# The first stage of a hybrid encoder layer written anew: halved first weights, squares behind the next chunk's high halves, additions on VectorE, memory tokens split directly

## The chip, the cores and the metric

The kernel runs on 1 core of one Trainium2 chip. The metric is the device time of one execution in microseconds (us), the median of the runs. The engines are named as in the profile: PE is TensorE (matmuls; PEld its weight loads), DVE VectorE, ACT ScalarE, POOL GpSimd, SP the engine whose queue issues most of the DMAs.

## What is computed

One step of an encoder layer for a prompt of 1024 frames and 8 samples of 16 frames, together 1152 tokens of width 1024, all in float32:

```python
h = rmsnorm(x, p['g_pre1'])              # x * rsqrt(mean(x*x) + 1e-6) * g
z = h @ p['w_in']                        # (1152, 1024) @ (1024, 1024)
u_ssm, u_pool, q_mem = z[..., :512], z[..., 512:768], z[..., 768:]
y_ssm, ... = s5_scan(u_ssm, ...)         # complex diagonal state space
y_pool, ... = multiscale_pool(u_pool, ...)
y_mem = memory_attention(q_mem, mk, mv)
gates = sigmoid(h @ p['w_gate'] + p['b_gate'])       # three branches
x = x + rmsnorm((gates * branches @ w_br).sum() @ p['w_out'], p['g_post1'])
x = x + rmsnorm(conv_ffn(rmsnorm(x, p['g_pre2']), ...), p['g_post2'])

def memory_kv(mem, g_mem, w_mem_k, w_mem_v):         # 256 memory tokens
    mn = rmsnorm(mem, g_mem)
    return mn @ w_mem_k, mn @ w_mem_v
```

The change touches the first RMS norm, the first columns of `z`, and `memory_kv` of the prompt.

## The kernel before

Every float32 operand of a matmul is split into a high half and a low half (`whi`, `wlo` for weights, `hhi`, `hlo` for tokens, `mhi`, `mlo` for memory tokens). The high half is an ACT copy into the type that PE multiplies, the low half is the difference, made on DVE as a rule. `mm3` (L101) makes one product from three matmuls: high by high (L103), weights' high by tokens' low (L106), weights' low by tokens' high (L107).

The tokens lie as features by tokens: 8 tiles of 128 features, in three chunks of 384 tokens. `z_tile(w, c)` (L195) makes 128 columns of `z` for chunk `c`: 8 feature tiles, 24 matmuls of 128x384, in one bank of PSUM. There are four banks called `pc` and four called `ps`.

The norm's gain `g` is put into the tokens when they are split: `feat_split` (L122) makes `hhi` on ACT (L126) and `hlo` on DVE (L127), a feature tile at a time. The norm's factor is put in after the matmul. `feat_sq` (L134) squares a chunk in four pieces of 128x768 (L140 on ACT, L142 on POOL if its letter in `engs` is "G"), adds them in pairs (L144, on POOL), adds the two sums (L148) and the halves of that (L149) on DVE; `feat_cols` (L153) sums over features with six matmuls by a column of ones (L156). `rsqrt` (L80) takes the root (ACT L84, POOL L86), `row_bcast` (L89) makes three diagonal matrices on ACT (L94) and spreads them by matmul (L96), ACT copies that to `rb` (L177), and `scaled` (L198) multiplies a finished tile of `z` by it on DVE (L200), whereupon `done` writes it out by DMA.

`start` (L262) is the first stage: it loads the tokens in 12 pieces (L165) and the weights of columns 0, 1 and 2, makes the nine `z` tiles of them, the three chunks' factors, and then the memory tokens' keys, the tiles of columns 3 (`z(3)`) and the memory tokens' values. Chunk 0's sums are called `q0`, chunk 1's `q1`, chunk 2's `q2`. `mem_split` (L217) multiplies the memory tokens by their gain on POOL (L224), copies the high half on ACT (L63) and subtracts on POOL (L64). Beside it stands `ssm_params` (from L339), many small DVE operations on the state-space parameters (called `pr` in the profile, L356 to L506), which the scheduler sets between the rest.

The order on each engine is made by a scheduler from its own estimate of times. The program steers it in three ways: `keep_in_program_order` (`pin=True`) holds a matmul at its written place among the pinned ones, `high_priority` brings work forward, and `issue_after(i)` keeps all work in its block behind instruction `i`. The raw weights have 3 buffers, the split weights 6, and the squares share 2 buffers of tag `U` and one each of `CA` and `V`.

Of the kernel before, what the change touches and what calls it, by code (L numbers as in the profile page):

```python
# [8 lines left out]
F32R = mybir.dt.float32r  # L9
# [12 lines left out]
V_GPRE1, V_GPRE2, V_GMEM, V_BGATE, V_BGLU = 0, 8, 16, 24, 48  # L22
# [10 lines left out]
class K:  # L33
# [67 lines left out]
    def mm3(self, out, whi, wlo, xhi, xlo, start, stop, pin=False):  # L101
        nc = self.nc
        i = nc.tensor.matmul(out, whi, xhi, start=start, stop=False)  # L103
        if pin:
            self.tc.keep_in_program_order(i)
        nc.tensor.matmul(out, whi, xlo, start=False, stop=False)  # L106
        nc.tensor.matmul(out, wlo, xhi, start=False, stop=stop)  # L107
# [26 lines left out]
    def feat_sq(self, P, x, n, tags, engs="AAAA", add=True):  # L134
        nc = self.nc
        sq = [P.tile([128, 2, n * 128], F32, tag=t, name="sq") for t in tags]
        for a in range(4):
            xa = x[:, 2 * a:2 * a + 2]
            if engs[a] == "A":
                nc.scalar.activation(sq[a], xa, AF.Square)  # L140
            else:
                (nc.vector if engs[a] == "V" else nc.gpsimd).tensor_mul(sq[a], xa, xa)  # L142
            if a % 2:
                nc.gpsimd.tensor_add(sq[a - 1], sq[a - 1], sq[a])  # L144
        parts = [sq[i][:, k] for i in (0, 2) for k in range(2)]
        if add:
            with self.tc.high_priority():
                nc.vector.tensor_add(sq[0], sq[0], sq[2])  # L148
                nc.vector.tensor_add(parts[0], parts[0], parts[1])  # L149
            parts = parts[:1]  # L150
        return parts
# [64 lines left out]

    def mem_split(self, x):  # L217

        nc = self.nc
        mhi = self.mtile([128, 8, 256], F32R, "mhi")  # L220
        mlo = self.mtile([128, 8, 256], F32R, "mlo")
        for a in range(2):
            ks = slice(4 * a, 4 * a + 4)
            nc.gpsimd.tensor_mul(x[:, ks], x[:, ks],  # L224
                                 self.vec[:, V_GMEM + 4 * a:V_GMEM + 4 * a + 4, None].to_broadcast([128, 4, 256]))
            self.split(mhi[:, ks], mlo[:, ks], x[:, ks], nc.gpsimd)
        return mhi, mlo

    def mem_rows(self, P, rs):
# [32 lines left out]
    def start(self, P, pair, done, z):  # L262
        nc = self.nc
        self.hhi, self.hlo = [], []
        sh = (128, 4, 256)
        I = self.I
        x0 = self.h_load(0, (0,))
        rw = [self.load_raw(I["w_in"][pair[0]])]
        self.h_load(0, (1, 2, 3), x0)
        rw.append(self.load_raw(I["w_in"][pair[1]]))  # L270
        x1 = self.h_load(1)
        x2 = self.h_load(2)
        tags = ("U", "U", "CA", "V")
        ss = self.sm()

        def rms(c0, n):
            with self.tc.high_priority():
                return self.rsqrt(P, ss[:, c0:c0 + n], n)

        self.h_tiles()  # L280
        a, v = self.h_split(x0, (0, 1))
        w = [self.load_w(None, r=rw[0])]
        lo, up = range(4), range(4, 8)
        with self.tc.issue_after(a.ins), self.tc.issue_after(v.ins):
            self.h_split(x0, range(2, 8))
            b0 = [self.z_tile(w[0], 0, pin=True)]
            w.append(self.load_w(None, r=rw[1]))
            q0 = self.feat_sq(P, x0, 3, tags, "AGAA")
        self.h_tiles()
        self.h_split(x1)  # L290
        b0.append(self.z_tile(w[1], 0, pin=True))
        t = self.pc()
        self.z_tile(w[0], 1, t, lo, True)
        self.feat_cols(q0, 3, ss[:, 0:3], True)
        b1 = [self.z_tile(w[0], 1, t, up, True)]
        b1.append(self.z_tile(w[1], 1, pin=True))
        self.h_tiles()
        self.h_split(x2, lo)
        self.h_rows(P, rms(0, 3), 0, True)
        with self.tc.issue_after(self.diag.ins):  # L300
            self.h_split(x2, up)
            for i in range(2):
                done(pair[i], 0, b0[i])
            q1 = self.feat_sq(P, x1, 3, tags, add=True)
            t = self.sm()
            self.z_tile(w[0], 2, t, lo, True)
            self.feat_cols(q1, 3, ss[:, 3:6], True)
            b2 = [self.z_tile(w[0], 2, t, up, True)]
            t = self.pc()
            self.z_tile(w[1], 2, t, lo, True)  # L310
            self.h_rows(P, rms(3, 3), 1, True)
            b2.append(self.z_tile(w[1], 2, t, up, True))
            for i in range(2):
                done(pair[i], 1, b1[i])
        with self.tc.issue_after(self.diag.ins):
            w2 = self.load_w(I["w_in"][2])
            q2 = self.feat_sq(P, x2, 3, tags, "AAAA")
            done(2, 0, self.z_tile(w2, 0, pin=True))
            self.feat_cols(q2, 3, ss[:, 6:9], True)
            done(2, 1, self.z_tile(w2, 1, pin=True))  # L320
            b = self.z_tile(w2, 2, pin=True)
            self.h_rows(P, rms(6, 3), 2, True)
            d = self.diag
            for i in range(2):
                done(pair[i], 2, b2[i])
            done(2, 2, b)
            xm = self.mem_load()
            wk = [self.load_w(I["w_mk"][h], sh) for h in range(2)]
            self.feat_sums(P, xm, 2, ss[:, 9:11], tags, "AAAA")
            mem = self.mem_split(xm)  # L330
            rsm = self.mem_rows(P, rms(9, 2))
            self.mem_out(P, "mk", self.mem_kv(mem, "mk", wk), *rsm)
            z(3)
            wv = [self.load_w(I["w_mv"][h], sh) for h in range(2)]
            self.mem_out(P, "mv", self.mem_kv(mem, "mv", wv), *rsm)
        return d
# [1500 lines left out]
```

## Time and profile before

| | |
|---|---|
| median of 3 runs | 1626.8 us (1624.13 to 1631.04) |
| the profiled execution | 1622.7 us, its span 1620.9 us |
| mean granted clock of PE | 0.979 |
| busy: PE, DVE | 1558.3 us (96%), 1031.3 us (64%) |
| busy: ACT, POOL | 586.2 us (36%), 586.3 us (36%) |
| DMA | 163.44 MB, mean 101 GB/s |

The span is the time between the first and the last instruction that the profiler saw. A row of a timeline reads: start, length (both us), engine, line, operation, output and inputs by the program's names, shapes, count; in brackets the idle time of the engine before the row and what ended it. A row of the groups gives the count, the busy time in us and the mean of one in ns.

### The profile page before, as it was taken

To read this page: it belongs to the slowest core of one execution; us is meant where nothing else is said; L and a number is where in the kernel's file an instruction comes from. 1 tells how busy PE (TensorE), PEld (TensorE's weight loads), DVE (VectorE), ACT (ScalarE), POOL (GpSimd) and SP (SyncE) were. 2 spreads that over 40 slices of the span, in tenths; PEclk is the share of its full clock that TensorE was granted. 3 is DMA by queue.
4 is the path that set the end of the run, shared out by engine and by line. 5 is a ranking of instruction groups with operands and counts; after the bars stand their busy time and mean duration, and the time that the engine had idled before them with its cause. 6 is when DMAs were issued, how large, how long until landed. Compare 5 with 4: busy or idle time off the path is not lost.

```text
span 1620.9 us, 22934 instructions
## 1 busy us (share of the span) xinstructions
PE 1558.3 (96%) x8964; PEld 1511.3 (93%) x8964; DVE 1031.3 (64%) x1549; ACT 586.2 (36%) x893; POOL 586.3 (36%) x509
## 2 busy tenths in 40 slices
PE   6899999999999999999879999999999999999996
PEld 5899999868899999998879999999999998999996
DVE  7864987645643354624678655555655658788866
ACT  6322444253321242434445333433333333332321
POOL 2400001000011143326666444534443426655546
PEclk9899999999999999999879999999999999999998
DMA  6343334413232235122323221212121233133214
GB/s 245 100 146 95 107 114 145 150 64 121 95 117 81 71 80 162 56 96 76 122 88 129 76 75 62 82 69 81 54 82 69 82 135 122 51 110 103 91 64 166
DMA packets 98460, 163.44 MB, mean 101 GB/s; under 512 B 23216, under 2 KB 68656, under 8 KB 98352
## 3 DMA queue, kind: packets, MB, share of 16 engines
q1 hardware_dynamic: 97920, 161.75, 30.3%
q8 instruction: 70, 1.15, 0.3%
q14 instruction: 38, 0.31, 0.1%
q10 hardware_dynamic: 432, 0.23, 0.0%
HBM read 119.52 MB, written 42.42 MB: 100 GB/s over the span
## 4 chain that ended last, share of the span: by engine, by line
PE 79%; DVE 9%; issue 3%; DMA 3%; ACT 2%; POOL 1%; POOLq 0%; SPq 0%; DVEq 0%; ACTq 0%
PE pc L107 14%; PE pc L103 14%; PE pc L106 14%; PE ps L103 10%; PE ps L106 10%; PE ps L107 10%; PE ps L842 1%; DVE dB L64 1%; DMA Ts<-DG 1%; POOL ssa L1057 1%; DVE wlo L64 1%; PE ps L1065 1%; DMA DG<-gs 1%; DMA dwr<-in_w_down 1%; DVE mg L1095 1%
## 5 line engine op out<-in xcount | busy, mean ns | idle before, releaser
L103 PE MATMUL pc<-hhi,whi 128*128 128x384 f32 x760 | 259.9, 342 | 7.7 <-ACT hhi L126 7.6
L106 PE MATMUL pc<-hlo,whi 128*128 128x384 f32 x760 | 260.7, 343 | 2.6 <-DVE hlo L127 2.6
L107 PE MATMUL pc<-hhi,wlo 128*128 128x384 f32 x760 | 257.7, 339 | 0.5 <-DVE wlo L64 0.5
L63 ACT ACTIVATE whi<-rawt 128x1024 fp32r<-128x1024 f32 x102 | 107.5, 1055 | 180.7 <-PE pc L106 80.7
L64 DVE TENSOR_TENSOR wlo<-rawt,whi 128x1024 fp32r<-128x1024 f32 x102 | 131.9, 1295 | 56.9 <-ACT whi L63 56.3
L103 PEld LDWEIGHTS pc<-hhi,whi 128*128 128x128 f32 x760 | 144.8, 191 | 10.3 <-ACT hhi L126 7.6
L106 PEld LDWEIGHTS pc<-hlo,whi 128*128 128x128 f32 x760 | 144.7, 190 | 7.4 <-DVE hlo L127 3.5
L107 PEld LDWEIGHTS pc<-hhi,wlo 128*128 128x128 f32 x760 | 144.6, 190 | 3.2 <-issue 1.6
L200 DVE TENSOR_TENSOR sg<-pc,rb 128x384 f32<-128x384 f32 x95 | 52.3, 553 | 122.7 <-PE pc L107 120.2
L107 PE MATMUL pc<-h2hi,wlo 128*128 128x384 f32 x352 | 119.1, 338 | 2.1 <-DVE wlo L64 2.0
L103 PE MATMUL pc<-h2hi,whi 128*128 128x384 f32 x352 | 118.3, 336 | 0.0
L106 PE MATMUL pc<-h2lo,whi 128*128 128x384 f32 x352 | 118.2, 336 | 0.0
L64 DVE TENSOR_TENSOR S<-S,S 128x512 fp32r<-128x512 f32 x85 | 75.9, 895 | 64.2 <-ACT S L63 62.2
L63 ACT ACTIVATE S<-S 128x512 fp32r<-128x512 f32 x88 | 55.1, 629 | 160.2 <-PE ps L107 89.8
L917 ACT ACTIVATE sg<-sg,vec 128x384 f32<-128x384 f32 x72 | 44.1, 613 | 148.2 <-DVE sg L200 121.2
L1004 POOL TENSOR_TENSOR mg<-mg,sgl 128x384 f32<-128x384 f32 x24 | 28.2, 1174 | 171.9 <-DVE sgl L1002 168.6
L103 PE MATMUL ps<-bT,S 128*128 128x384 f32 x240 | 80.2, 334 | 0.0
L106 PE MATMUL ps<-bT,S 128*128 128x384 f32 x240 | 80.2, 334 | 0.0
L107 PE MATMUL ps<-bT,S 128*128 128x384 f32 x240 | 80.2, 334 | 0.0
L1237 POOL TENSOR_TENSOR S<-rawt 128x512 f32<-128x512 f32 x22 | 29.8, 1355 | 125.9 <-PE ps L107 124.3
L63 ACT ACTIVATE dhi<-dwr 128x1024 fp32r<-128x1024 f32 x38 | 39.7, 1058 | 95.9 <-PE pc L106 61.4
L107 PEld LDWEIGHTS pc<-h2hi,wlo 128*128 128x128 f32 x352 | 66.1, 188 | 2.8 <-DVE wlo L64 2.8
(458 smaller groups left out, 4401.0 us busy)
## 6 DMA issues: line engine op xcount, KB each, us to landing
rawt<-in_w_up SPq DMA_DIRECT2D x48, 512.0 KB, 3.3
Dact<-t SPq DMA_DIRECT2D x22, 576.0 KB, 3.5
rawt<-in_w_gate SPq DMA_DIRECT2D x24, 512.0 KB, 3.5
dwr<-in_w_down SPq DMA_DIRECT2D x22, 512.0 KB, 3.5
Dsg<-sg SPq DMA_DIRECT2D x45, 192.0 KB, 1.9
sgl<-Dsg SPq DMA_DIRECT2D x45, 192.0 KB, 2.4
dBr<-Dact SPq DMA_DIRECT2D x8, 768.0 KB, 5.7
xT<-in_xT SPq DMA_DIRECT2D x12, 384.0 KB, 7.6
```

The source lines that it names most:

```text
L63: nc.scalar.activation(hi, src, AF.Copy)
L64: (eng or nc.vector).tensor_sub(lo, src, hi)
L103: i = nc.tensor.matmul(out, whi, xhi, start=start, stop=False)
L106: nc.tensor.matmul(out, whi, xlo, start=False, stop=False)
L107: nc.tensor.matmul(out, wlo, xhi, start=False, stop=stop)
L200: self.nc.vector.tensor_mul(sg, b, self.rb[:, c, :])
L842: nc.tensor.matmul(o, va[:, m, 2 * hp + e, :], pT[:, m, :], start=m == 0, stop=m == 1)
L917: self.nc.scalar.activation(sg, sg, AF.Sigmoid, bias=self.vec[:, V_BGATE + m:V_BGATE + m + 1])
L1004: nc.gpsimd.tensor_add(m, m, sp)
L1057: self.sqadd = G.tensor_add(ss[0], ss[0], sq)
L1065: m = nc.tensor.matmul(s3[:, t:t + 1], s[:, t * 128:t * 128 + 128], self.ones[:, 0:1], start=(i, t) == (0, 0), stop=(i, t) == (len(ss) - 1 ...
L1237: G.tensor_sub(s3, a11, a21)
```

## The change

Five things, all in the first stage. The numbers of lines after the change are two higher from about L270 on.

- The pair additions of the squares (L144) go from POOL to DVE, and all squares of chunk 0 to ACT.
- The memory tokens are split by `feat_split`, as the others are: eight ACT copies with the gain as scale and eight DVE operations of 128x256, and no multiplication by the gain ahead of them.
- The first weights come in two DMAs of four feature tiles each, and are split in two halves, each followed by four feature tiles of chunk 0.
- The squares of a chunk stand behind all high halves of the next chunk, by `issue_after`; before, chunk 0's stood between its own high halves.
- The blocks of `issue_after` are drawn anew: nearly the whole stage stands in the first one, and the memory tokens behind the diagonal of row 1.

```diff
@@ -141,7 +141,7 @@
             else:
                 (nc.vector if engs[a] == "V" else nc.gpsimd).tensor_mul(sq[a], xa, xa)
             if a % 2:
-                nc.gpsimd.tensor_add(sq[a - 1], sq[a - 1], sq[a])
+                nc.vector.tensor_add(sq[a - 1], sq[a - 1], sq[a])
         parts = [sq[i][:, k] for i in (0, 2) for k in range(2)]
         if add:
             with self.tc.high_priority():
@@ -216,14 +216,9 @@
 
     def mem_split(self, x):
 
-        nc = self.nc
         mhi = self.mtile([128, 8, 256], F32R, "mhi")
         mlo = self.mtile([128, 8, 256], F32R, "mlo")
-        for a in range(2):
-            ks = slice(4 * a, 4 * a + 4)
-            nc.gpsimd.tensor_mul(x[:, ks], x[:, ks],
-                                 self.vec[:, V_GMEM + 4 * a:V_GMEM + 4 * a + 4, None].to_broadcast([128, 4, 256]))
-            self.split(mhi[:, ks], mlo[:, ks], x[:, ks], nc.gpsimd)
+        self.feat_split(x, mhi, mlo, V_GMEM, range(8))
         return mhi, mlo
 
     def mem_rows(self, P, rs):
@@ -265,7 +260,10 @@
         sh = (128, 4, 256)
         I = self.I
         x0 = self.h_load(0, (0,))
-        rw = [self.load_raw(I["w_in"][pair[0]])]
+        halves = slice(0, 4), slice(4, 8)
+        rw = [self.rawtile([128, 8, 128])]
+        for hs in halves:
+            nc.sync.dma_start(rw[0][:, hs], I["w_in"][pair[0]][:, hs])
         self.h_load(0, (1, 2, 3), x0)
         rw.append(self.load_raw(I["w_in"][pair[1]]))
         x1 = self.h_load(1)
@@ -279,42 +277,45 @@
 
         self.h_tiles()
         a, v = self.h_split(x0, (0, 1))
-        w = [self.load_w(None, r=rw[0])]
+        w = [[self.w1.tile([128, 8, 128], F32R, tag="w", name=n) for n in ("whi", "wlo")]]
+        self.split(w[0][0][:, halves[0]], w[0][1][:, halves[0]], rw[0][:, halves[0]])
         lo, up = range(4), range(4, 8)
         with self.tc.issue_after(a.ins), self.tc.issue_after(v.ins):
-            self.h_split(x0, range(2, 8))
+            self.h_split(x0, (2, 3))
+            self.split(w[0][0][:, halves[1]], w[0][1][:, halves[1]], rw[0][:, halves[1]])
+            self.h_split(x0, up)
             b0 = [self.z_tile(w[0], 0, pin=True)]
             w.append(self.load_w(None, r=rw[1]))
-            q0 = self.feat_sq(P, x0, 3, tags, "AGAA")
-        self.h_tiles()
-        self.h_split(x1)
-        b0.append(self.z_tile(w[1], 0, pin=True))
-        t = self.pc()
-        self.z_tile(w[0], 1, t, lo, True)
-        self.feat_cols(q0, 3, ss[:, 0:3], True)
-        b1 = [self.z_tile(w[0], 1, t, up, True)]
-        b1.append(self.z_tile(w[1], 1, pin=True))
-        self.h_tiles()
-        self.h_split(x2, lo)
-        self.h_rows(P, rms(0, 3), 0, True)
-        with self.tc.issue_after(self.diag.ins):
-            self.h_split(x2, up)
+            self.h_tiles()
+            a, _ = self.h_split(x1)
+            b0.append(self.z_tile(w[1], 0, pin=True))
+            with self.tc.issue_after(a.ins):
+                q0 = self.feat_sq(P, x0, 3, tags)
+            t = self.pc()
+            self.z_tile(w[0], 1, t, lo, True)
+            self.h_tiles()
+            a, _ = self.h_split(x2)
+            self.feat_cols(q0, 3, ss[:, 0:3], True)
+            b1 = [self.z_tile(w[0], 1, t, up, True)]
+            b1.append(self.z_tile(w[1], 1, pin=True))
+            with self.tc.issue_after(a.ins):
+                q1 = self.feat_sq(P, x1, 3, tags)
+            self.h_rows(P, rms(0, 3), 0, True)
             for i in range(2):
                 done(pair[i], 0, b0[i])
-            q1 = self.feat_sq(P, x1, 3, tags, add=True)
             t = self.sm()
             self.z_tile(w[0], 2, t, lo, True)
             self.feat_cols(q1, 3, ss[:, 3:6], True)
             b2 = [self.z_tile(w[0], 2, t, up, True)]
+            q2 = self.feat_sq(P, x2, 3, tags)
             t = self.pc()
             self.z_tile(w[1], 2, t, lo, True)
             self.h_rows(P, rms(3, 3), 1, True)
+            behind = self.tc.issue_after(self.diag.ins)
             b2.append(self.z_tile(w[1], 2, t, up, True))
             for i in range(2):
                 done(pair[i], 1, b1[i])
-        with self.tc.issue_after(self.diag.ins):
             w2 = self.load_w(I["w_in"][2])
-            q2 = self.feat_sq(P, x2, 3, tags, "AAAA")
             done(2, 0, self.z_tile(w2, 0, pin=True))
             self.feat_cols(q2, 3, ss[:, 6:9], True)
             done(2, 1, self.z_tile(w2, 1, pin=True))
@@ -324,12 +325,13 @@
             for i in range(2):
                 done(pair[i], 2, b2[i])
             done(2, 2, b)
-            xm = self.mem_load()
-            wk = [self.load_w(I["w_mk"][h], sh) for h in range(2)]
-            self.feat_sums(P, xm, 2, ss[:, 9:11], tags, "AAAA")
-            mem = self.mem_split(xm)
-            rsm = self.mem_rows(P, rms(9, 2))
-            self.mem_out(P, "mk", self.mem_kv(mem, "mk", wk), *rsm)
+            with behind:
+                xm = self.mem_load()
+                wk = [self.load_w(I["w_mk"][h], sh) for h in range(2)]
+                self.feat_sums(P, xm, 2, ss[:, 9:11], tags, "AAAA")
+                mem = self.mem_split(xm)
+                rsm = self.mem_rows(P, rms(9, 2))
+                self.mem_out(P, "mk", self.mem_kv(mem, "mk", wk), *rsm)
             z(3)
             wv = [self.load_w(I["w_mv"][h], sh) for h in range(2)]
             self.mem_out(P, "mv", self.mem_kv(mem, "mv", wv), *rsm)
```

ACT from its start. Before, with a square (L140) after every few high halves of chunk 0:

```order
L63 ACTIVATE whi<-rawt 128x1024
L126 ACTIVATE hhi<-xT,vec 128x384 x4
L140 ACTIVATE sq<-xT 128x768
L126 ACTIVATE hhi<-xT,vec 128x384 x2
L140 ACTIVATE sq<-xT 128x768
L126 ACTIVATE hhi<-xT,vec 128x384 x2
L140 ACTIVATE sq<-xT 128x768
L63 ACTIVATE whi<-rawt 128x1024
L126 ACTIVATE hhi<-xT,vec 128x384 x12
```

ACT from its start, after:

```order
L63 ACTIVATE whi<-rawt 128x512
L126 ACTIVATE hhi<-xT,vec 128x384 x4
L63 ACTIVATE whi<-rawt 128x512
L126 ACTIVATE hhi<-xT,vec 128x384 x4
L63 ACTIVATE whi<-rawt 128x1024
L126 ACTIVATE hhi<-xT,vec 128x384 x8
L140 ACTIVATE sq<-xT 128x768 x4
L126 ACTIVATE hhi<-xT,vec 128x384 x8
L140 ACTIVATE sq<-xT 128x768
```

The first weights' split is in two parts, and chunk 0's four squares have moved behind all eight high halves of chunk 1.

DVE from its start, before, up to chunk 0's sum (L149):

```order
L64 TENSOR_TENSOR wlo<-rawt,whi 128x1024
L127 SCALAR_TENSOR_TENSOR hlo<-xT,vec,hhi 128x384 x8
L64 TENSOR_TENSOR wlo<-rawt,whi 128x1024
L127 SCALAR_TENSOR_TENSOR hlo<-xT,vec,hhi 128x384
L148 TENSOR_TENSOR sq<-sq 128x768
L127 SCALAR_TENSOR_TENSOR hlo<-xT,vec,hhi 128x384 x4
L149 TENSOR_TENSOR sq<-sq 128x384
```

DVE from its start, after, up to the same sum:

```order
L64 TENSOR_TENSOR wlo<-rawt,whi 128x512
L127 SCALAR_TENSOR_TENSOR hlo<-xT,vec,hhi 128x384 x4
L64 TENSOR_TENSOR wlo<-rawt,whi 128x512
L127 SCALAR_TENSOR_TENSOR hlo<-xT,vec,hhi 128x384 x4
L64 TENSOR_TENSOR wlo<-rawt,whi 128x1024
L127 SCALAR_TENSOR_TENSOR hlo<-xT,vec,hhi 128x384 x8
L144 TENSOR_TENSOR sq<-sq 128x768 x2
L127 SCALAR_TENSOR_TENSOR hlo<-xT,vec,hhi 128x384 x2
L148 TENSOR_TENSOR sq<-sq 128x768
L127 SCALAR_TENSOR_TENSOR hlo<-xT,vec,hhi 128x384 x3
L371 COPY pr_841<-par 128x16
L149 TENSOR_TENSOR sq<-sq 128x384
```

The two pair additions are new on DVE, and the sum stands behind 21 low halves instead of 13.

DVE ahead of the low half of the weights of `z(3)` (the `wlo` that is followed by a `sg<-ps,rb`), before:

```order
L148 TENSOR_TENSOR sq<-sq 128x512
L149 TENSOR_TENSOR sq<-sq 128x256
L503 TENSOR_TENSOR CA<-pr_879,bc 128x576
L506 TENSOR_TENSOR CA<-pr_879,bc 128x576
L200 TENSOR_TENSOR sg<-pc,rb 128x384
L64 TENSOR_TENSOR wlo<-rawt,whi 128x1024
L200 TENSOR_TENSOR sg<-ps,rb 128x384
```

DVE at the same place, after:

```order
L495 TENSOR_TENSOR ar_952<-pr_892,bc 128x512
L498 TENSOR_TENSOR ar_952<-pr_892,bc 128x512
L505 TENSOR_TENSOR CA<-pr_892,bc 128x576
L508 TENSOR_TENSOR CA<-pr_892,bc 128x576
L473 TENSOR_TENSOR wa<-ar_952 128x8
L407 TENSOR_TENSOR pr_892<-pr_897,pr_898 128x64
L474 TENSOR_TENSOR wb<-ar_952 128x8
L614 TENSOR_TENSOR sd<-pr_892,h_946 128x32
L64 TENSOR_TENSOR wlo<-rawt,whi 128x1024
L200 TENSOR_TENSOR sg<-ps,rb 128x384
```

More of the parameters' work stands ahead of that `wlo`, and the memory tokens' sum has moved farther ahead.

On POOL the first stage has, before, the square, eight additions L144, two L224 and two L64; after, only the four rows L86 are left of it. SP issues two DMAs of 128x512 for the first weights in the place of one.

## The prediction

> **What bounds the kernel now.** I read the page's busy times first, then the windows by 100 us, then the waits of TensorE in the first 120 us, then the timelines of TensorE and VectorE there.
>
> ```profile
> PE 1558.3 (96%) x8964; PEld 1511.3 (93%) x8964; DVE 1031.3 (64%) x1549; ACT 586.2 (36%) x893; POOL 586.3 (36%) x509
> ...
> 0.00:100.00 100.00, 79.81 (x436) 76.70 (x437) 85.29 (x218) 48.27 (x84) 32.68 (x36) 0.95 0.53 179
> 100.00:200.00 100.00, 99.83 (x702) 99.00 (x700) 63.88 (x166) 29.91 (x49) 5.08 (x22) 1.00 0.32 101
> ```
>
> The columns of a window are PE, PEld, DVE, ACT, POOL, granted clock, DMA share and GB/s. PE is the bound, 96% of the span. In the first 100 us it is busy for 79.81 only, and in the next 100 for 99.83: behind the first stage PE never waits, so what the first stage gives or takes is carried to the end one for one. Inside it VectorE (DVE) is the busiest, 85.29. Whom PE waits for (total, times, longest), and the three long rows:
>
> ```profile
> PE ps L156 <- DVE sq L149: 9.3, 2, 4.8
> PE pc L103 <- ACT hhi L126: 7.6, 1, 7.6
> PE pc L106 <- DVE hlo L127: 2.6, 2, 1.9
> PE pc L107 <- DVE wlo L64: 0.5, 1, 0.5
> ```
>
> ```profile
> 39.42 1.44 PE L156 MATMUL ps<-ones,sq 128*128 128x1 f32 x6 [4.78 <-DVE sq L149]
> ...
> 58.76 1.13 PE L156 MATMUL ps<-ones,sq 128*128 128x1 f32 x6 [4.55 <-DVE sq L149]
> ...
> 72.42 0.44 PE L107 MATMUL pc<-hhi,wlo 128*128 128x384 f32 x1 [0.52 <-DVE wlo L64]
> ```
>
> Every wait but the first is for DVE. After each the granted clock is low:
>
> ```profile
> 7.60:18.10 10.50, 7.84 (x22) 6.94 (x23) 10.50 (x11) 10.50 (x19) 4.84 (x3) 1.00 1.03 404
> 39.40:45.50 6.10, 6.08 (x21) 6.08 (x22) 5.78 (x36) 3.60 (x8) 0.89 (x1) 0.50 0.06 16
> 58.80:62.60 3.80, 3.80 (x15) 3.80 (x16) 0.29 (x2) 2.51 (x6) 2.42 (x3) 0.55 0.16 47
> ```
>
> At half clock I take half of the time for lost: 2.8 of the second stretch (less the first small matmuls) and 1.7 of the third. In the first the 22 matmuls need half of the 7.84, so some 4.0 are lost. Waits 20.0 (9.3 + 7.6 + 2.6 + 0.5) and clock 8.5 make 28.5 us, all that this stage can give.
>
> **The change: what DVE gains.** DVE's own rows show why it is late. Beside some of them a GpSimd (POOL) addition or multiplication runs, and then a row lasts until that one ends:
>
> ```profile
> 7.10 2.48 DVE L64 TENSOR_TENSOR wlo<-rawt,whi 128x1024 fp32r<-128x1024 f32 x1 [6.19 <-ACT whi L63]
> ...
> 31.48 1.75 DVE L371 TENSOR_TENSOR pr<-par,pr 128x16 f32<-128x16 f32 x1
> 33.16 0.16 DVE L374 TENSOR_TENSOR pr<-par,pr 128x16 f32<-128x16 f32 x1
> 33.27 1.78 DVE L356 TENSOR_SCALAR pr<-pr 128x16 f32<-128x16 f32 x1
> ...
> 45.96 1.88 DVE L400 TENSOR_TENSOR pr<-pr 128x64 f32<-128x64 f32 x1
> 47.76 1.88 DVE L401 TENSOR_TENSOR pr<-pr 128x64 f32<-128x64 f32 x1
> 49.67 0.23 DVE L402 TENSOR_TENSOR pr<-pr,pr 128x64 f32<-128x64 f32 x1
> ...
> 51.60 0.68 DVE L494 TENSOR_TENSOR tg<-pr,bc 128x512 f32<-128x512 f32 x1
> ...
> 55.24 1.25 DVE L614 TENSOR_TENSOR sd<-sd 128x32 f32<-128x32 f32 x1
> ...
> 56.88 1.83 DVE L149 TENSOR_TENSOR sq<-sq 128x384 f32<-128x384 f32 x1
> ...
> 62.32 2.37 DVE L148 TENSOR_TENSOR sq<-sq 128x512 f32<-128x512 f32 x1 [3.51 <-POOL sq L144]
> 64.72 2.50 DVE L149 TENSOR_TENSOR sq<-sq 128x256 f32<-128x256 f32 x1
> 67.15 2.95 DVE L503 TENSOR_TENSOR CA<-pr,bc 128x576 f32<-128x576 f32 x1
> 70.02 0.75 DVE L506 TENSOR_TENSOR CA<-pr,bc 128x576 f32<-128x576 f32 x1
> ...
> 71.16 1.21 DVE L64 TENSOR_TENSOR wlo<-rawt,whi 128x1024 fp32r<-128x1024 f32 x1
> ```
>
> ```profile
> 31.36 3.65 POOL L144 TENSOR_TENSOR sq<-sq 128x768 f32<-128x768 f32 x2 [4.66 <-DVE pr L363]
> ...
> 64.10 5.39 POOL L64 TENSOR_TENSOR mlo<-mem,mhi 128x1024 fp32r<-128x1024 f32 x2
> ```
>
> L371 starts just behind POOL's first addition and L356 ends at 35.05, POOL's second at 35.01; the same shape takes 0.16 at 33.16. POOL's last large row ends at 69.49, and L503's long row at 70.10. The change takes from POOL every such row of this stage (additions L144, square L142, L224 and L64 of the memory tokens). Stalls that go, each row less its undisturbed like: first wlo 2.48 - 1.21 = 1.27; L371 1.59; L356 1.62 (0.16); L400 and L401 2 x 1.65 = 3.3; L614 1.25 - 0.2 = 1.05; L149 1.83 - 0.55 = 1.28 (between 0.42 for 256 and 0.68 for 512); L148 1.69; second L149 2.50 - 0.42 = 2.08; L503 2.20. And the low halves:
>
> ```profile
> 42.30 0.42 DVE L436 TENSOR_TENSOR tm<-bc,pr 128x256 f32<-128x256 f32 x1
> ```
>
> ```profile
> L127 DVE SCALAR_TENSOR_TENSOR hlo<-xT,vec,hhi 128x384 fp32r<-128x384 f32 x24 | 16.5, 736 | 1.1 <-ACT hhi L126 1.1
> ```
>
> ```profile
> 28.88 0.61 DVE L127 SCALAR_TENSOR_TENSOR hlo<-xT,vec,hhi 128x384 fp32r<-128x384 f32 x1
> ```
>
> 24 x (0.736 - 0.61) = 3.0. Together 19.1. Two waits of DVE go too: 3.51 for POOL at 62.32 and 1.1 for ACT's high halves, since the squares no longer stand between them: 4.6. The first weights come in halves: 256 KB at the 404 GB/s of the first stretch land 0.65 earlier, and ACT's split of a half is about 0.45 shorter than this:
>
> ```profile
> 6.01 1.06 ACT L63 ACTIVATE whi<-rawt 128x1024 fp32r<-128x1024 f32 x1 [3.56 <-DMA rawt<-in_w_in]
> ```
>
> So DVE starts 1.1 earlier. Gone from DVE's queue up to the wlo that PE awaits at 72.42: 19.1 + 4.6 + 1.1 = 24.8.
>
> **What DVE gets.** A row starts 0.07 before the one ahead of it ends, so it costs its duration less 0.07. Six pair additions of 128x768 by this row, 0.87 each, are 5.2:
>
> ```profile
> 18.56 0.94 DVE L148 TENSOR_TENSOR sq<-sq 128x768 f32<-128x768 f32 x1
> ```
>
> Two of 128x512 (0.68) are 1.2, eight low halves of the memory tokens (128x256, 0.42 to 0.46, so 0.39) 3.1: 9.5. The order puts some work of the state-space parameters ahead of that wlo that stood behind it: one more 128x512 (0.6), four copies and 12 small operations less three: 13 at 0.09 to 0.21, 1.8 to 3.3 in all; I take 2.4. DVE now waits for squares that ACT makes behind eight high halves, and for the memory tokens' high halves, which stand on ACT behind row 1's diagonal: nothing to 3, I take 1.6. The wlo ends at 72.37 - 24.8 + 9.5 + 2.4 + 1.6 = 61.1, 11.3 earlier, and PE gets there some 3.0 before it, a longer wait than the 0.52 of before.
>
> **The same from PE's side.** First matmul 6.5 instead of 7.6. Its first waits for low halves go from 2.6 to about 0.4. The 22 matmuls of the first window took 7.84, 0.36 each at half clock with a few long ones; I take 0.33, and 0.17 at full clock. With the waits shorter the clock should rise after some 15 of them: 2.2 lost, not 4.0. L156 for chunk 0 comes after 60 matmuls: 6.5 + 0.4 + 15 x 0.33 + 45 x 0.17 = 19.5. There PE did not wait before, and now it does, since ACT's four squares stand behind chunk 1's eight high halves:
>
> ```profile
> 14.16 6.18 ACT L126 ACTIVATE hhi<-xT,vec 128x384 fp32r<-128x384 f32 x12
> ...
> 29.65 3.03 ACT L140 ACTIVATE sq<-xT 128x768 f32<-128x768 f32 x4
> ```
>
> ACT starts at 6.01 - 0.65, and two half splits (0.5 each), one whole (1.0) and 16 high halves (0.51 each) take it to 15.5; four squares (0.75 each) end at 18.6. DVE then does the addition, L148, L149 and five low halves between them (0.9 + 0.9 + 0.5 + 5 x 0.54, and a copy), to 23.7: a new wait of 4.2, and behind it a half-clock stretch, 1.7 to 2.8 by the two rows above, 2.2. For chunks 1 and 2 the sums are ready before PE comes (DVE has them near 30 and 40, PE comes near 36 and 47), so 4.78 + 4.55 and both clock stretches go. What is lost after: 6.5 + 0.4 + 2.2 + 4.2 + 2.2 + 3.0 = 18.5, against 28.5: 10.0 gained. The two sums give 11.3 and 10.0. The first goes by the queue that ends last; from it I take 0.5 for a half-clock stretch behind the wait of 3.0 (0 to 1.7): **10.8**.
>
> What costs nothing: the one more square on ACT, and eight ACT rows for two on the memory tokens (about 1.2 more), hidden since ACT is busy for 48.27 of 100; one more DMA on SP's queue, which delays the x pieces' issue by 0.4 under a stream that is full at 404 GB/s. If that cover is gone, each costs at most its own length, 2.8 in all. Behind the stage the engines' orders differ at one place, near 750 to 840 us, where PE waits now and then: 3 either way.
>
> The Trainium skill, "DMA: Bandwidth & Descriptors", section "Measured (HBM→SBUF, 128 partitions, SWDGE, issued from GpSimd)", tells authors to batch to 1 MiB or more, which speaks against halving the first load. Its 341 GB/s at 1 MB is below what this trace reaches with smaller pieces (404); by its figures for 64 KB and 1 MB a piece of 256 KB would come at about 180 GB/s, 0.8 us later, an estimate, and the time would be 1616.8.
>
> The profiled execution took 1622.7 (span 1620.9), so 1611.9 for one like it. The median of the runs, 1626.8, lies 4.1 above; the same gain from it gives **1616.0**.
>
> **Rivals.** First, the clock eats more. The wait for chunk 0's squares may cost two low stretches (2 x 2.8 = 5.6 for 2.2) and the wait of 3.0 a whole one (1.7 for 0.5): 10.8 - 3.4 - 1.2 = 6.2 gained, 1620.6, the same within what can be told. For it: short waits lowered the clock before, too:
>
> ```profile
> 761.30 0.91 PE L96 MATMUL ps<-diag,ones 128*128 128x384 f32 x2 [2.01 <-ACT diag L94]
> ```
>
> ```profile
> 762.30:765.70 3.40, 3.40 (x13) 3.40 (x12) 3.40 (x3) 0.33 (x1) 2.43 (x2) 0.50 0.00 0
> ```
>
> Against it: no low stretch of the first stage outlived 6.1 us once PE had work. Chance 0.22.
>
> Second, the other way: neither new wait lowers the clock. Then 2.2 + 0.5 come back, 13.5 gained, 1613.3. Against it stand the row at 761.30 (a wait of 2.01, then 0.50) and those at 39.42 and 58.76. Chance 0.10. The Trainium skill, "TensorE: Matmul & The Clock Gate", section "What's actually happening", says that the clock falls after an idle window of about 3.4 us; by that the wait of 3.0 could not lower it. The trace differs with its 2.01.
>
> Third, slower: the long rows are not POOL's doing but DVE's own queue or memory traffic, and stay. Then DVE loses 4.6 + 1.1 and gains 13.5: the wlo ends 7.8 later, a low stretch (1.7) behind it, +9.5, 1636.3. It decides once fewer than 7.8 of the 19.1 go. Against it: the ends of L371, L356 and L503 fall on POOL's. Chance 0.06.
>
> **How the numbers follow.** Forecast 0.62, rivals 0.22, 0.10 and 0.06. A difference under 0.5%, 8.1 us, can't be told from none. Below 1618.7 lie the forecast (of 0.62 some 0.06 reaches above, where the small costs add up) and the second rival: faster 0.56 + 0.10 = 0.66, same 0.22 + 0.06 = 0.28, slower 0.06. The range is 1609 to 1624: downwards the second rival and 3 of the later order, and the runs' own spread; upwards the first with 3. It leaves out the third and ends.
>
> **What would show it.** On POOL only small rows before 75 us; L371, L356, L400, L401, L503 at their short durations; the first matmul near 6.5; waits at L156 of 4 to 5 for chunk 0 and none for the others; a wait for wlo of about 3 near 60. Wrong if DVE's long rows remain, if the clock stays at half beyond 30 us, or if PE in 100 to 200 us is no longer full, so that the gain is given back.

## The result and the profile after

| | before | after |
|---|---|---|
| median (4 runs each) | 1625.53 us (1624.13 to 1631.04) | 1608.65 us (1606.98 to 1609.30) |
| profiled execution, span | 1622.7, 1620.9 us | 1609.0, 1607.2 us |
| PE, DVE busy | 1558.3, 1031.3 us | 1552.8, 1017.8 us |

The change makes the kernel faster, by 1.1%: ratio 0.9888, 95% interval 0.9863 to 0.9914. Measured once more it was 0.9903 (0.9887 to 0.9919). The forecast was 1616.0 with a range of 1609 to 1624: the sign and the mechanism in the first stage came true, the gain is larger than forecast, and the time lies 0.35 below the range. Two executions of the later experiments (1729.6 and 2555.67 us, at granted clocks of 0.839 and 0.556) are in no ratio.

The windows of the changed kernel, 0 to 100, 100 to 200, the start, and what follows the wait for chunk 0's sum and the wait for the low half of `z(3)` (columns as before: PE, PEld, DVE, ACT, POOL, granted clock, DMA share, GB/s):

```profile
0.00:100.00 100.00, 86.82 (x502) 84.75 (x503) 84.51 (x270) 51.48 (x93) 8.76 (x23) 0.97 0.57 190
100.00:200.00 100.00, 99.82 (x702) 98.96 (x702) 64.24 (x148) 32.12 (x53) 5.19 (x22) 1.00 0.32 99
6.40:11.80 5.40, 5.32 (x16) 4.86 (x17) 4.71 (x10) 4.59 (x9) 0.00 (x0) 1.00 1.02 398
24.50:28.80 4.30, 4.30 (x16) 4.30 (x17) 4.13 (x10) 3.83 (x9) 1.10 (x1) 0.50 0.94 330
61.10:67.90 6.80, 6.80 (x44) 6.75 (x45) 6.80 (x24) 1.08 (x3) 0.00 (x0) 1.00 0.80 207
```

In the third row, the start, the clock's column shows 1.00, but the 16 matmuls took 5.32, 0.33 each; on PE's timeline they start 0.32 apart from 7.7 to 11.5 us and 0.17 apart from 11.8 on. For the start the length of the matmuls has to be read, not that column.

PE gained 7.0 us of work in the first 100 us, and is full behind it as before. POOL went from 32.68 to 8.76. The list of PE's waits in the first 120 us is down to three, and its timeline has the three sums and the last low half:

```profile
PE pc L103 <- ACT hhi L126: 6.4, 1, 6.4
PE ps L156 <- DVE sq L149: 4.7, 1, 4.7
PE pc L107 <- DVE wlo L64: 2.0, 1, 2.0
```

```profile
24.49 1.41 PE L156 MATMUL ps<-ones,sq 128*128 128x1 f32 x6 [4.70 <-DVE sq L149]
...
36.24 0.72 PE L156 MATMUL ps<-ones,sq 128*128 128x1 f32 x6
...
47.96 0.72 PE L156 MATMUL ps<-ones,sq 128*128 128x1 f32 x6
...
61.08 0.44 PE L107 MATMUL pc<-hhi,wlo 128*128 128x384 f32 x1 [2.00 <-DVE wlo L64]
```

Chunk 0's sum is waited for anew, those of chunks 1 and 2 no more. On DVE the rows that POOL had stretched are short (its timeline, then its groups up to 61 us):

```profile
23.80 0.55 DVE L149 TENSOR_TENSOR sq<-sq 128x384 f32<-128x384 f32 x1
...
34.10 0.17 DVE L373 TENSOR_TENSOR pr<-par,pr 128x16 f32<-128x16 f32 x1
...
55.26 0.21 DVE L402 TENSOR_TENSOR pr<-pr 128x64 f32<-128x64 f32 x1
...
58.08 0.75 DVE L505 TENSOR_TENSOR CA<-pr,bc 128x576 f32<-128x576 f32 x1
...
59.81 1.21 DVE L64 TENSOR_TENSOR wlo<-rawt,whi 128x1024 fp32r<-128x1024 f32 x1
```

```profile
L127 DVE SCALAR_TENSOR_TENSOR hlo<-xT,vec,hhi 128x384 fp32r<-128x384 f32 x24 | 13.4, 610 | 0.7 <-ACT hhi L126 0.7
...
L144 DVE TENSOR_TENSOR sq<-sq 128x768 f32<-128x768 f32 x6 | 5.7, 957 | 1.5 <-ACT sq L140 1.5
L127 DVE SCALAR_TENSOR_TENSOR mlo<-mem,vec,mhi 128x256 fp32r<-128x256 f32 x8 | 3.7, 479 | 0.8 <-ACT mhi L126 0.8
```

L373 was L371 with 1.75, L505 was L503 with 2.95, the low halves took 0.736 each and now 0.610. The last `wlo` ends at 61.02; the forecast's sum gave 61.1.

### The profile page after: what moved, and what is told of

It reads as the page before. It is cut to its first block, busy times and chain, and to the rows that moved or that the text cites. A ratio compares the mean times of both kernels' runs of the same rounds, so it can differ in the third digit from the quotient of the medians.

```text
span 1607.2 us, 22947 instructions
## 1 busy us (share of the span) xinstructions
PE 1552.8 (97%) x8964; PEld 1507.0 (94%) x8964; DVE 1017.8 (63%) x1566; ACT 587.7 (37%) x901; POOL 560.7 (35%) x496
## 4 chain that ended last, share of the span: by engine, by line
PE 79%; DVE 10%; DMA 4%; issue 3%; ACT 2%; POOL 1%; SPq 0%; POOLq 0%; DVEq 0%; ACTq 0%
PE pc L107 14%; PE pc L103 14%; PE pc L106 14%; PE ps L103 10%; PE ps L106 10%; PE ps L107 10%; DVE dB L64 1%; PE ps L844 1%; DMA Ts<-DG 1%; DMA xT<-in_xT 1%; DMA DG<-gs 1%; POOL ssa L1059 1%; DVE wlo L64 1%; DMA dwr<-in_w_down 1%; PE ps L1067 1%
## 5 line engine op out<-in xcount | busy, mean ns | idle before, releaser
L103 PE MATMUL pc<-hhi,whi 128*128 128x384 f32 x760 | 259.7, 342 | 6.4 <-ACT hhi L126 6.4
L106 PE MATMUL pc<-hlo,whi 128*128 128x384 f32 x760 | 260.6, 343 | 0.1
L107 PE MATMUL pc<-hhi,wlo 128*128 128x384 f32 x760 | 258.0, 340 | 2.0 <-DVE wlo L64 2.0
L63 ACT ACTIVATE whi<-rawt 128x1024 fp32r<-128x1024 f32 (+1 forms) x103 | 107.7, 1046 | 186.8 <-PE pc L106 81.9
L64 DVE TENSOR_TENSOR wlo<-rawt,whi 128x1024 fp32r<-128x1024 f32 (+1 forms) x103 | 129.4, 1258 | 57.4 <-ACT whi L63 56.7
L103 PEld LDWEIGHTS pc<-hhi,whi 128*128 128x128 f32 x760 | 144.9, 191 | 8.6 <-ACT hhi L126 6.4
L107 PEld LDWEIGHTS pc<-hhi,wlo 128*128 128x128 f32 x760 | 144.6, 190 | 4.9 <-DVE wlo L64 2.3
L106 PEld LDWEIGHTS pc<-hlo,whi 128*128 128x128 f32 x760 | 144.6, 190 | 4.4 <-issue 3.0
L107 PE MATMUL pc<-h2hi,wlo 128*128 128x384 f32 x352 | 119.1, 338 | 2.2 <-DVE wlo L64 2.1
L103 PE MATMUL pc<-h2hi,whi 128*128 128x384 f32 x352 | 118.3, 336 | 0.0
L106 PE MATMUL pc<-h2lo,whi 128*128 128x384 f32 x352 | 118.2, 336 | 0.0
L64 DVE TENSOR_TENSOR S<-S,S 128x512 fp32r<-128x512 f32 x85 | 72.6, 857 | 64.3 <-ACT S L63 62.3
L103 PE MATMUL ps<-bT,S 128*128 128x384 f32 x240 | 80.2, 334 | 0.0
L106 PE MATMUL ps<-bT,S 128*128 128x384 f32 x240 | 80.2, 334 | 0.0
L107 PE MATMUL ps<-bT,S 128*128 128x384 f32 x240 | 80.2, 334 | 0.0
L107 PEld LDWEIGHTS pc<-h2hi,wlo 128*128 128x128 f32 x352 | 66.1, 188 | 2.8 <-DVE wlo L64 2.8
```

The costliest lines, as they stand in the source:

```text
L63: nc.scalar.activation(hi, src, AF.Copy)
L64: (eng or nc.vector).tensor_sub(lo, src, hi)
```

## Where the time went, by three landmarks

To follow a difference through the kernel I use rows that stand once in every trace. Landmark A is ACT's table load ahead of L630 of before, at 189.41; B is PE's L96 behind the wait of 2.01, at 761.30; C is ACT's table load for the GELU, at 863.85. Before and after, on ACT's timeline:

```profile
189.41 1.28 ACT L630 ACT_TABLE_LOAD   x1
...
863.85 1.28 ACT L1303 ACT_TABLE_LOAD   x1
```

```profile
178.06 1.28 ACT L632 ACT_TABLE_LOAD   x1
...
849.41 1.28 ACT L1305 ACT_TABLE_LOAD   x1
```

A moves by -11.4, the first stage's part. From B (after: 750.96) to C the stage took 102.6 before and 98.5 after: 4.1 more, where the prediction had 0 with 3 either way. What is left, +1.8 of the span's -13.7, lies elsewhere: between A and B the changed kernel's trace has one half-clock stretch more (363 to 367 us, granted clock 0.57), some 1.7 by that clock. The same numbers for every kernel that ran, with its ratio to the kernel before (A as its difference to the first trace of before; B to C as the length of that stage):

| kernel | ratio, 95% interval | A | B to C |
|---|---|---|---|
| before, again | 1.0002 (0.9989 to 1.0014) | +0.9 | 102.4 |
| changed, first trace | 0.9888 (0.9863 to 0.9914) | -11.4 | 98.5 |
| changed, again | 0.9903 (0.9887 to 0.9919) | -8.3 | 98.3 |
| before + halved first weights | 0.9969 (0.9958 to 0.9980) | -0.8 | 98.6 |
| changed + idle GpSimd additions | 0.9940 (0.9926 to 0.9955) | -5.2 | 98.4 |
| before + additions on VectorE | 0.9991 (0.9978 to 1.0005) | -2.2 | 99.9 |
| before + memory split directly | 0.9975 (0.9959 to 0.9990) | -0.1 | 98.2 |
| before + both of these | 0.9954 (0.9939 to 0.9970) | -6.4 | 101.5 |
| changed, additions on GpSimd | 0.9961 (0.9946 to 0.9975) | -1.1 | 99.3 |
| before, one row moved at 810 us | 0.9978 (0.9966 to 0.9991) | -0.8 | 99.1 |
| changed, chunk 0's sum later | 0.9909 (0.9893 to 0.9924) | -12.7 | 102.5 |
| changed, memory split on GpSimd | 0.9977 (0.9965 to 0.9989) | -2.2 | 101.0 |
| changed, sum and row 0 later, row at 810 us | 0.9882 (0.9864 to 0.9900) | -16.6 | 98.4 |

Two traces of one kernel differ by about 1 at A where nothing was changed, and by up to 3 where a half-clock stretch comes or stays away. All but the two main kernels have a single trace, so a difference of 1 at A can be chance.

## The experiments

**Both kernels again.** No edit; five rounds each.

> The changed kernel once more, to see what of its 16.9 us is the program and what is one execution's chance. Theory order: the stage from 750 to 850 us is shorter by 4 because the engines' order there has changed, so this trace shows the same 4 again, a span of 1605 to 1609 and a ratio of 0.988 to 0.990. Theory chance: those 4 us come from where the half-clock stretches happen to fall, so this execution shows another value there, anywhere from 0 to 5.

> The kernel before once more. Its first profiled execution took 1622.7 where the median of its runs is 1625.5. Theory order: the stage from 750 to 850 us takes the same time as in the first trace, within 1 us. Theory chance: it differs by 2 us or more, and the spread of the runs (1622.7 to 1631.0) comes from there.

Median 1609.18 against 1626.01 for 20 runs of the kernel before (1621.78 to 1630.38); the kernel before again 1625.71. Both stages B to C repeat within 0.2 (102.6 and 102.4; 98.5 and 98.3): the 4 us there are the program's, not chance. They do not follow PE's clock either: from B to C it is 0.83 and 0.87 in the two traces of before, and 0.86 in both of the changed kernel. What is chance showed elsewhere. The second trace of the changed kernel has the same wait for the last low half, with another clock behind it; PE's row, and the window, whose clock is 0.50 where the first trace had 1.00:

```profile
61.71 0.69 PE L107 MATMUL pc<-hhi,wlo 128*128 128x384 f32 x1 [1.99 <-DVE wlo L64]
```

```profile
61.70:67.90 6.20, 6.19 (x19) 6.19 (x20) 6.10 (x20) 0.69 (x2) 0.00 (x0) 0.50 0.71 201
```

Half of 6.2 is 3.1, and A differs by as much (-8.3 for -11.4). The prediction gave this stretch 0 to 1.7. From C to the end the second trace of the kernel before is 3.8 longer (760.9 against 757.1), most of the 4.2 us between the two spans. It has a wait of 2.5 near 1550 us there that the first had not, and a granted clock of 0.90 from 1545 to 1562:

```profile
PE ps L103 <- ACT act L63: 2.5, 1, 2.5
```

**Halved first weights alone**, on the kernel before:

```diff
+        for hs in halves:
+            nc.sync.dma_start(rw[0][:, hs], I["w_in"][pair[0]][:, hs])
...
+        self.split(w[0][0][:, halves[0]], w[0][1][:, halves[0]], rw[0][:, halves[0]])
```

> The kernel before with one part of the change alone: the first weights in two DMAs and two splits. In this build the first stage keeps the order of before apart from that, while the engines' order near 750 to 850 us is that of the changed kernel. Theory order: first matmul 1.1 earlier, first stage 1 to 2 shorter, and 4 more gained at 750 to 850: span near 1615, ratio 0.996 to 0.997. Theory chance: the first stage's 1 to 2 alone, 1619 with 3 either way.

A gains 0.8 (1 to 2 expected), no more than the two traces of before differ by; the first matmul starts at 6.76, 0.9 earlier. B to C gains 3.9: a first stage in the old order, with the new order at 800 us, has the 4 us. This speaks for order.

**One row moved at 810 us**, and nothing of the change:

```diff
-            op("T4", h0[:, up], G)
+            t4 = op("T4", h0[:, up], G)
...
+        with self.tc.issue_after(behind.ins) if behind else ExitStack():
+            G.tensor_sub(s3, a11, a21)
+            G.tensor_sub(s4, a12, s2)
```

> The kernel before with nothing of the change in its first stage, and with one row moved near 810 us: GpSimd's second subtraction for bT (128x1536) stands ahead of the two additions for S, as the changed kernel's order has it. Theory order: TensorE's wait of 2.1 for that row goes, the stage from 750 to 850 us is 1.5 to 3 shorter, the first stage is unchanged; time 1623 to 1624.5, against 1626.0. Theory chance: nothing moves, 1625 to 1627.

Ratio 0.9978, B to C 99.1 instead of 102.6: 3.5 gained where 1.5 to 3 were expected (the medians differ by 3.0). The program moved a single row; one square on ACT (L1053) changed its place with it. POOL's timeline before, and with the row moved:

```profile
811.89 2.37 POOL L86 TENSOR_TENSOR rs_y<-rs_v,mhalf 128x3 f32<-128x3 f32 x1
815.87 1.29 POOL L1237 TENSOR_TENSOR S<-rawt 128x512 f32<-128x512 f32 x1 [1.60 <-PE pc L107]
817.11 1.29 POOL L1238 TENSOR_TENSOR S<-rawt,S 128x512 f32<-128x512 f32 x1
818.35 4.43 POOL L64 TENSOR_TENSOR bT<-mg,bT 128x1536 fp32r<-128x1536 f32 x1
```

```profile
811.28 2.38 POOL L86 TENSOR_TENSOR rs_y<-rs_v,mhalf 128x3 f32<-128x3 f32 x1
813.63 3.50 POOL L64 TENSOR_TENSOR bT<-mg,bT 128x1536 fp32r<-128x1536 f32 x1
817.10 2.26 POOL L1238 TENSOR_TENSOR S<-rawt 128x512 f32<-128x512 f32 x1
```

Before, POOL idled 1.60 for PE with the ready subtraction queued behind, and PE then waited for that subtraction:

```profile
822.84 0.45 PE L106 MATMUL pc<-bT,whi 128*128 128x384 f32 x1 [2.08 <-POOL bT L64]
```

With the row moved that wait is gone. How the 3.5 divides between waits and clock can't be read: between B and C all of PE's waits come to 18.5 with the row moved, against 17.8 and 21.0 in the two traces of before, and its busy time to 82.4, against 86.6 and 83.3. Every build in the table with 98 to 99.3 from B to C, but for the memory split alone, whose order there is a third one, has this row moved; those with 101 to 102.6 have not. The additions on VectorE alone have not either, and stand at 99.9; why stays open. The orders of ACT and DVE in this stage also differ between these builds, so only the run with this one row bears on it alone.

**Idle additions on GpSimd** beside the changed kernel:

```diff
...
+                    for k in range(2):
+                        nc.gpsimd.tensor_add(self.dm, sq[a][:, k], sq[a][:, k])
```

> The changed kernel with two additions of 128x384 on GpSimd beside each of the six pair additions of the tokens' squares; they read the squares and write a scratch tile that nobody reads, so no instruction waits for them. Theory of the prediction (GpSimd's additions stretch VectorE's rows): each pair stretches the VectorE rows beside it by 1 to 2 us, the low half of the weights of z(3) ends some 5 later, at 66, and the time is 3 to 6 above the changed kernel. Rival (VectorE was late by its dependencies and its queue): nothing moves, the rows beside the dummies keep 0.95, time within 1 of the changed kernel.

Nothing reads what they write, yet DVE's rows are stretched, in turns with POOL's (DVE's timeline, then POOL's):

```profile
28.55 0.95 DVE L144 TENSOR_TENSOR sq<-sq 128x768 f32<-128x768 f32 x1
29.42 0.81 DVE L365 TENSOR_SCALAR pr<-pr 128x16 f32<-128x16 f32 x1
30.14 0.95 DVE L144 TENSOR_TENSOR sq<-sq 128x768 f32<-128x768 f32 x1
31.01 0.81 DVE L366 SCALAR_TENSOR_TENSOR pr<-pr,pr 128x16 f32<-128x16 f32 x1
```

```profile
29.26 5.50 POOL L149 TENSOR_TENSOR dm<-sq 128x384 f32<-128x384 f32 x4
```

The small rows take 0.81 for 0.17; the pair additions keep 0.95, other than expected (one sum of the same shape, at 21.95, took 1.58). The last `wlo` ends at 65.16, 4.1 later (5 expected). A is 6.1 worse than in the first trace of the changed kernel and 3.0 worse than in the second. The ratio is 0.9940 against 0.9903, timed together: 6 us. One thing did wait: a square on ACT, at 34.79, waited 1.1 for an addition to let go of its buffer. It does not explain DVE's delay, since DVE's waits for squares are 0.5 in this trace and 1.5 in the changed kernel's. The rival, a queue late by its dependencies, falls.

**The two parts that free GpSimd**, each and together on the kernel before (the additions' line, and `mem_split` by `feat_split`, as in the diff of the change):

> The kernel before with one part alone: the pair additions of the squares on VectorE. Theory GpSimd stretches VectorE: L371, L356, L400 and L401 fall to 0.16 to 0.23, the two waits for the sums at L156 (9.3 in all) fall to about 6, the stage up to 100 us is 2 to 4 shorter. Rival (the gain lies in the new order of squares and halves): no more than 1. Near 750 to 850 us this build has one of the two order changes (the ACT one near 770), worth about 2. Together 1620 to 1622 by the first, 1623 to 1624 by the rival.

> The kernel before with one part alone: the memory tokens split directly, on ACT and VectorE. Reading by sums, as the prediction added them up: the long rows at 62 to 70 us (L148, L149, L503) shrink by 6 and eight rows of 0.39 come in, so 3 are gained. Reading by place: TensorE's waits for the sums of chunks 1 and 2 come earlier, at 39 and 59 us, and stay; the last low half has to wait for TensorE's own L106 at 69 us anyway; so nothing is gained in the first stage, 0 to 1. Time 1623 by sums, 1625 to 1626 by place.

> Both parts together on the kernel before: GpSimd has no large row left in the first stage, while the squares, the first weights and the blocks stand as before. If freeing GpSimd is most of the gain, 6 to 8 of the 10 us of the first stage appear here, with waits of about 3 each at the two sums and 1 at the last low half; if the new order is most of it, 3 or less. With 2 from the order near 770 us: 1616 to 1618 by the first, 1621 or more by the second.

The additions alone give 2.2 at A; the memory tokens alone 0.1; both 6.4. For the additions alone the time decides nothing (0.9991, with 1 in its interval), but the rows do: L371 and L356 take 0.17, L400 and L401 0.21, and the waits at L156 are 4.5 for 9.3, with a new one of 2.7 for the last low half. The reading by place is right for the memory tokens: alone they give nothing at A. PE's waits come before (39.18 and 58.25, still 5.01 and 4.57). Their ratio below 1 comes from B to C (98.2). Freed of the earlier waits, the same rows are worth 4. The waits with both, in the first 100 us:

```profile
PE pc L103 <- ACT hhi L126: 7.5, 1, 7.5
PE ps L156 <- DVE sq L149: 6.7, 2, 4.2
PE pc L106 <- DVE hlo L127: 1.9, 1, 1.9
PE pc L107 <- DVE wlo L64: 0.7, 2, 0.4
```

So 6.4 of the first stage's 8.3 to 11.4 come from freeing GpSimd, which has one square (L142, 1.47) and the small rows L86 left here. The rest comes with the earlier start and the squares' new place, which take away 2.0 of the waits at L156, 1.9 at L106 and 1.1 at L103, and add 1.3 at L107.

**Each put back** into the changed kernel:

> The changed kernel with the pair additions put back on GpSimd. Theory GpSimd stretches VectorE: TensorE's wait for chunk 0's sum grows from 4.7 to about 6.8, new waits of 2 to 3 come up behind it for VectorE's multiplications by rb, the first stage is 6 to 9 longer; time 1615 to 1619. Rival (the order is what gained): 0 to 3 longer, 1609 to 1612.

> The changed kernel with the memory tokens split on GpSimd as before (two multiplications and two subtractions of 128x1024), VectorE adding the squares. Theory GpSimd stretches VectorE: the rows beside them grow, TensorE waits some 3 more for a sum and 3 for the low half of z(3), the first stage is 4 to 7 longer, and one of the two order changes near 800 us is lost (2): 1614 to 1618. Rival: 0 to 1 longer, 1609 to 1612.

Additions back: A is 7 to 10 worse than in the two traces of the changed kernel (6 to 9 expected), the wait for chunk 0's sum 6.9 (6.8 expected), and a wait of 2.5 for DVE's multiplication by `rb` comes up. Memory tokens back: A is 6 to 9 worse, more than the 4 to 7 expected, with the time 3 above its interval: the waits are as foreseen (2.7 for a sum, 3.4 for the last low half), but the clock stays low over both of them, 0.53 from 61 to 72 us. DVE beside POOL's two subtractions (POOL's row first):

```profile
53.02 4.98 POOL L64 TENSOR_TENSOR mlo<-mem,mhi 128x1024 fp32r<-128x1024 f32 x2
```

```profile
53.13 2.62 DVE L447 TENSOR_TENSOR bc<-bc,pr 128x256 f32<-128x256 f32 x1
55.67 2.62 DVE L445 TENSOR_TENSOR bc<-bc,pr 128x256 f32<-128x256 f32 x1
```

Rows of 0.42 take 2.62, and the second ends 0.3 behind POOL's second. With the additions back, a row with a single tile as input is held in the same way (POOL's row, then DVE's):

```profile
26.41 2.25 POOL L144 TENSOR_TENSOR sq<-sq 128x768 f32<-128x768 f32 x1 [5.04 <-ACT sq L140]
```

```profile
26.92 1.78 DVE L358 TENSOR_SCALAR pr<-pr 128x16 f32<-128x16 f32 x1
```

The Trainium skill, "SBUF — State Buffer", section "SBUF: two separate sides", tells of an exclusive lock on a port pair that VectorE shares with GpSimd: a VectorE operation with two SBUF inputs against a GpSimd operation that reads SBUF, or one in a mode that uses both ports, and the later of the two is blocked until the other has ended; its section "Who interferes with whom" counts `tensor_scalar` among the operations that can enter such a mode. Both pairs of rows agree.

**Chunk 0's sum later**, to take the new wait away:

```diff
-            self.feat_cols(q0, 3, ss[:, 0:3], True)
             b1 = [self.z_tile(w[0], 1, t, up, True)]
             b1.append(self.z_tile(w[1], 1, pin=True))
+            self.feat_cols(q0, 3, ss[:, 0:3], True)
```

> The changed kernel with the sum for chunk 0 asked for 36 matmuls later, behind the z tiles of chunk 1, where it is ready. If TensorE's wait of 4.7 and the half clock behind it are on the path, 4 to 7 come back: 1603 to 1605. If VectorE's queue is the path, as the prediction had it, they turn up again at row 0's L96 (about 3) and at the low half of z(3) (about 3), and the first stage gains 0 to 1. This build has one of the two order changes near 800 us, so 2 must be added: 1609 to 1612 by the second.

The wait of 4.7 is gone, and 1.3 is gained at A against the first trace of the changed kernel (4.4 against the second), more than the 0 to 1 of the second expectation. As that one had it, a wait turned up again at row 0, and the last low half waits on:

```profile
PE pc L103 <- ACT hhi L126: 6.5, 1, 6.5
PE ps L96 <- ACT diag L94: 3.2, 1, 3.2
PE pc L107 <- DVE wlo L64: 2.5, 1, 2.5
```

The row at 810 us is back in its old place (102.5), so the time stays at 1610.4.

**A version meant to be better:** the same, with row 0's L96 behind the first half of chunk 2's tile, and the row at 810 us as in the changed kernel.

```diff
-            self.h_rows(P, rms(0, 3), 0, True)
-            for i in range(2):
-                done(pair[i], 0, b0[i])
             t = self.sm()
             self.z_tile(w[0], 2, t, lo, True)
+            self.h_rows(P, rms(0, 3), 0, True)
+            for i in range(2):
+                done(pair[i], 0, b0[i])
```

> A version meant to be better than both: chunk 0's sum asked for behind the z tiles of chunk 1, its row L96 behind the first half of chunk 2's tile, and the order near 810 us as in the changed kernel. The wait of 4.7 and its half clock go; the low half of z(3) must still follow TensorE's last L106 of column 2 and VectorE's queue, so a wait of 3 to 4 stands there. 2 to 4 below the changed kernel: 1605 to 1607. If VectorE's queue alone decides, the same as the changed kernel, 1608 to 1610.

1605.98 us (1604.39 to 1607.61), ratio 0.9882 (0.9864 to 0.9900), against 1608.65 and 1609.18, 0.9888 and 0.9903 for the changed kernel: faster in its median by some 3, as expected, though the intervals overlap and the runs were not timed together. A moved by 5.2 against the first trace; the last low half's matmul starts at 55.76 instead of 61.08, so DVE's queue was not a floor of its own: with other matmuls ahead, the scheduler put other rows behind that low half (L495 to L508, four of 128x512 and 128x576). Its waits:

```profile
PE pc L103 <- ACT hhi L126: 6.5, 1, 6.5
PE pc L107 <- DVE wlo L64: 2.1, 1, 2.1
PE ps L96 <- ACT diag L94: 1.2, 1, 1.2
PE ps L156 <- DVE sq L149: 0.2, 1, 0.2
```

The waits come to 10.0, against 13.1 in the first trace of the changed kernel. The other 2.1 at A is what the half clock from 24.5 to 28.8 took in that trace (half of 4.3). Here the granted clock stays at 1.00 behind the start, although PE waited 1.2 and 2.1 (windows from 12 to 30 and from 30 to 60 us):

```profile
12.00:30.00 18.00, 16.80 (x98) 16.09 (x96) 17.21 (x33) 17.40 (x34) 1.20 (x1) 1.00 0.97 350
30.00:60.00 30.00, 27.67 (x158) 26.27 (x157) 29.37 (x136) 16.24 (x35) 2.57 (x3) 1.00 0.37 109
```

## Why the prediction was right or wrong

- That GpSimd's additions stretch VectorE's rows: right, and shown both ways (idle additions added, parts put back). The third rival, with its stalls that stay, falls.
- The `wlo` at 61.1: 61.02. The first matmul at 6.5: 6.42. The new wait of 4.2 at L156: 4.70, from 19.8 to 24.49 (forecast 19.5 to 23.7). No wait for chunks 1 and 2: right. The wait of 3.0 for the last low half: 2.00. That the `wlo` agrees to 0.1 is partly luck: up to there DVE waited 3.0 behind its first row (1.5, 0.8 and 0.7) where the sum had 1.6, so the sum's other terms were too long by as much.
- That the stalls add up along DVE's queue: right in the sum, wrong as a way to price one part. The memory tokens' share alone was worth nothing until the waits ahead of it were gone.
- "After each the granted clock is low": the first of the three windows shown under it has 1.00. That the matmuls ran slowly there is read from their length (22 in 7.84), not from the clock; the forecast of 15 slow ones after the change was right (16 in 5.32).
- The half-clock stretch behind the last wait, "0 to 1.7", taken as 0.5: mis-sized. It was 0 in one trace and 3.1 in the other, behind the same wait of 2.0. The second rival's clock came half true: no fall there in the first trace, but one behind the wait for chunk 0's sum in both (0.50 for 4.3 us). The Trainium skill, "TensorE: Matmul & The Clock Gate", section "What's actually happening", says that the window over which the clock is decided runs freely and does not start with the kernel; two executions that differ behind one and the same wait agree with it. Its idle window of 3.4 us as the condition does not: 1.99 was enough once.
- "Behind the stage the engines' orders differ at one place ... 3 either way": this is the first step that failed. The difference was seen and priced at nothing in the middle. It gave 4.1, and most of it comes with one row (3.5 by its trace, 3.0 by the medians), for which PE's wait (2.08 at 822.84) stood in the trace of before. With 0.6 more at A than the 10.8 forecast, and 1.8 lost elsewhere, it makes the 2.9 by which the profiled execution (1609.0) beat its forecast (1611.9).
- "The median of the runs, 1626.8, lies 4.1 above; the same gain from it gives 1616.0": this is the other, and the larger, 4.4 of the 7.35. The offset belonged to one execution. The first trace of before, at 1622.7, lies near the low end of a spread of 1621.8 to 1630.4; the changed kernel's profiled execution lies 0.3 above its median. So the medians gained 16.8 to 16.9 where the first two traces gained 13.7 and the second two 16.5. The 20 executions of before spread over 8.6 us, the nine of the changed kernel over 3.5; why is not shown. An offset of one execution can't be carried over to another program.

## What to carry to other kernels

Where VectorE is late, look in its rows for small operations that take as long as the GpSimd operation beside them; moving that work to VectorE can pay even though VectorE is the busier engine, and the gain comes only where a wait of TensorE hangs on it. When a scheduler orders the whole program, compare the order everywhere, and price each row that changes place at a wait that the trace already shows: here a change of the first 70 us moved a row at 810 us that was worth 3 to 3.5 us. And forecast the median from several executions, or say that one execution's distance from it is chance.

## What the runs showed of the hardware

- A VectorE operation of 16 elements a partition took about as long as the GpSimd operation that it met: 0.16 alone, 1.78 beside an addition of 128x768; one of 256 elements took 2.62 instead of 0.42 beside a subtraction of 128x1024. With short GpSimd operations (128x384) the engines took turns, and the small rows paid (0.81 each).
- The same TensorE wait of 2.0 us was followed by full clock in one execution and by 6.2 us at half clock in the next; in the last version one of 2.1 was followed by full clock.
- Two DMAs of 256 KB did not slow the first load: the first matmul came 1.2 earlier (0.9 with this part alone), at 398 GB/s in the first window.
